# Mixture of experts on float32 weights as loaded, two column halves of TensorE at a time

## The chip, the cores and the metric

The program runs on one core of one Trainium2 chip. Its time is device microseconds of that core, from launch to end; the profiled execution beside it is one run of the same program taken by the hardware profiler. All times below are microseconds (us) from the start of the span unless marked ns.

## The reference

Two blocks run over 256 tokens of width 1024. The first block is two layers of FFN, mixer and FFN. The second has a mixer (block attention and gated linear attention) and then the mixture of experts that this change is about:

```
logits = norm(x) @ w_router + b_router            # 32 experts, the 4 largest per token
for each expert e, on the tokens that chose it:
    h      = norm(x) @ w_exp_in[e] + b_exp_in[e]  # 1024 -> 2048, gate and linear units in turn
    g, u   = min(h[0::2], 7), clip(h[1::2], -7, 7)
    a      = g * sigmoid(1.702 g) * (u + 1)       # 1024
    y     += softmax weight * (a @ w_exp_out[e] + b_exp_out[e])   # 1024 -> 1024
out = final_norm(x + gate * y)
```

All numbers are float32, and the result must agree with a float32 computation closely. The weights of one expert are 12 MiB: 8 MiB in, 4 MiB out. 32 experts are 384 chunks of 1 MiB, 403 MB.

## The kernel before

All weights pass through one stream (class `Stream`): chunks of 128 partitions x 2048 float32 (1 MiB), issued on SP's queue into raw places, in the order in which TensorE will use them. `convert` splits half a chunk into two float32r parts that add up to it: ScalarE writes the high part `wh` (L284), VectorE the rest `wl` (L285). The parts stand in a ring of five pairs (pool `hl`). When the second half of a chunk is split, its raw place is free and `load` issues the next chunk into it.

In the dense stages both operands are split, and a product is three float32r products (`prod`, L347 to L349). In the experts each expert has 64 slots for tokens. `Group.gather` (L1475) picks the tokens of four experts by products with a one-hot matrix and keeps the high and low part of each slot side by side, so the stationary operand is 64 + 64 columns wide. `hidden` multiplies it with `wh` and `wl` of a quarter of the hidden units (L1536, L1537; 64 products per expert), which leaves the two parts of x in two halves of the PSUM rows. `folded` adds the halves while it transposes, with a product by two stacked identities (L1549); VectorE and ScalarE do the bias, the limits and the sigmoid; L1564 and L1565 split the result into `act`. `outputs` does the same with the second matrix (L1579, L1580; 32 products per expert), ScalarE copies the sum to `osb` (L1584), and `combine` (L1523) adds each token's weighted rows into four PSUM banks `y` with a float32 product.

The order is written out by hand: the loop over `q` emits one quarter of an expert's hidden units and one quarter of the outputs of an expert some five quarters earlier; `later(PRE, n, ...)` and `later(POST, n, ...)` put the copies and the small products n steps further on, before or after that step's conversions. Raw places: three (`raw`), four (`r0` to `r3`) that join before the last dense product, and two (`xth`, `xtl`) used once when the dense stage is over. Up to five half chunks of the first expert are converted while the dense stage still runs.

The router's own chain stands between the dense stage and the experts: norm, logits, the four largest, places, one-hot matrix, gather. After the last expert `gated_sum` (L1607, L1608), the last norm and two stores end the program.

Of the kernel before, what the change touches and what calls it, by code (L numbers as in the profile page):

```python
# [23 lines left out]
OUT_ORDER = [*range(4 * NE - 3), 4 * NE - 2, 4 * NE - 3, 4 * NE - 1]  # L24
# [3 lines left out]
# ---------------------------------------------------------------- weight stream  # L28
# [77 lines left out]
# ---------------------------------------------------------------- constants of the shapes  # L106
def constants():
    f = np.float32
    c = {}
# [38 lines left out]
    c["fold"] = np.concatenate([np.eye(64, dtype=f)] * 2)  # L148
# [5 lines left out]
# ---------------------------------------------------------------- data layout on the host  # L154
def cols(v):
    """[..., 128 n] -> [128, ..., n]: a vector as columns of 128."""
    v = np.asarray(v)
    return np.ascontiguousarray(np.moveaxis(v.reshape(*v.shape[:-1], -1, 128), -1, 0))


def layout(a):
    o = {}
    parts = []
    for ch in dense_chunks():
# [5 lines left out]
        a["w_exp_in_2"][0].reshape(NE, 2, 4, 128, 4, 256, 2).transpose(0, 4, 1, 3, 2, 6, 5)  # L170
    ).reshape(NE, 4, 2, 128, 2048)
    o["exp_out"] = np.ascontiguousarray(
        a["w_exp_out_2"][0].reshape(NE, 2, 4, 128, 2, 512).transpose(0, 4, 1, 3, 2, 5)
    ).reshape(NE, 2, 2, 128, 2048)
    o["exp_bias"] = np.ascontiguousarray(
        a["b_exp_in_2"][0].reshape(NE, 2, 4, 128, 2).transpose(3, 0, 1, 4, 2)).reshape(128, NE, 16)
# [24 lines left out]
# ---------------------------------------------------------------- the program  # L201
def build(tc, I, out):
# [26 lines left out]
    # persistent  # L229
# [22 lines left out]
    # ------------------------------------------------ weight stream  # L252
    class Stream:
        """Weight chunks: loaded whole, split into two exact float32r parts by halves, and given out by halves."""

        def __init__(self, chunks, raw, hl):
            self.ch, self.raw, self.hl = chunks, [(raw, "raw")] * RAW, [hl] * HL
            self.d = self.c = self.u = self.step = 0
            self.R, self.C = {}, {}
            self.pre, self.post = [], []  # L260
            self.side = self.units = None
            self.hold = False

        def load(self, parts=1):
            if self.d < len(self.ch):
                ap, w = self.ch[self.d]
                p, tag = self.raw[0]
                self.raw = self.raw[1:] + self.raw[:1]
                r = p.tile([128, 2048], FT, name="raw", tag=tag)
# [6 lines left out]
                self.d += 1  # L276

        def convert(self):
            i, h = divmod(self.c, 2)
            r, w = self.R[i], self.ch[i][1] // 2  # L280
            p = self.hl[self.c % len(self.hl)]
            hi = p.tile([128, 1024], FR, name="wh")
            lo = p.tile([128, 1024], FR, name="wl")
            A.activation(hi[:, :w], r[:, h * w:h * w + w], AF.Copy)  # L284
            V.tensor_tensor(lo[:, :w], r[:, h * w:h * w + w], hi[:, :w], OP.subtract)  # L285
            self.C[self.c] = (hi, lo)
            self.c += 1
            if h:
                del self.R[i]
                self.load()  # L290

        def more(self, p, tags, once=False):
            """Further places for raw chunks, filled at once and, unless once, again in their turn."""
            for tag in tags:
                self.raw.insert(0, (p, tag))
                self.load()
                if once:
                    self.raw.pop()

        def due(self, q):  # L300
            now = [f for n, f in q if n <= self.step]
            q[:] = [(n, f) for n, f in q if n > self.step]
# [3 lines left out]
        def later(self, q, n, f):  # L306
            q.append((self.step + n, f))
# [7 lines left out]
        def fill(self):  # L315
            while self.c < min(self.u + len(self.hl), 2 * len(self.ch)):
                self.convert()

        def get(self):
            self.step += 1  # L320
            self.due(self.pre)
            if not self.hold:
                self.fill()
            self.due(self.post)
            if self.u % 2 == 0:
                if self.units:
                    self.units.step()
# [23 lines left out]
    def mm_tok(ps, X, klist, w, last, mid=None):  # L351
        """ps[t] += X[k]^T W[k] for the k of a chunk; mid comes between the chunk's halves."""
# [11 lines left out]
    def wide(p, X, lo=0, hi=8):  # L364
        """p [128 outputs, 256 tokens] += W[k]^T X[k] for the k of half a chunk."""
# [5 lines left out]
    def rms_power(o, ss, scale, eps):  # L371
        """o = (ss * scale + eps) ** -0.5"""
# [17 lines left out]
    raw = enter("raw", RAW)  # L390
    hl = enter("hl", HL)
# [22 lines left out]
    # ---------------------------------------- side work of the first block, a piece per chunk  # L414
# [59 lines left out]
    # ---------------------------------------- natural -> transposed stationary parts  # L474
# [3 lines left out]
    def turned(src, k, n=2):  # L478
        """A bank with (src columns k .. k+n)^T, [128, n, 256]."""
# [7 lines left out]
    def make_xt(X, src, half, gcol=None, after=None):  # L487
        """X[k] = (src columns k)^T * gcol for the four k of a half."""
# [17 lines left out]
    def rms_of(ss, eps, name="rstd", pre=None):  # L506
        """(mean + eps) ** -0.5 from the halves' sums of squares, which pre scales first."""
# [8 lines left out]
    class Norm:  # L516
        """The normed, transposed x of the next stage, in two halves of the columns."""
# [18 lines left out]
    # ---------------------------------------- FFN  # L536
# [74 lines left out]
    # ---------------------------------------- units of softmax work, stepped between chunks  # L611
    class Steps:
        """Units under way take one stage per chunk, the oldest first; one new unit starts per chunk."""
# [12 lines left out]
        def finish(self):  # L626
            while self.step():
                pass
            st.units = None

    # ---------------------------------------- first mixer
    def mixer(l, norm, next_gain):
# [16 lines left out]
        # -- Fourier branch between the projections  # L649
# [17 lines left out]
        def row_rstd(dg):  # L667
            """rstd along the free dimension, on every partition"""
# [61 lines left out]
        # -- attention, in steps between the chunks of the values and the gates  # L730
# [53 lines left out]
        def diff_unit(h, qt):  # L784
# [39 lines left out]
            # the heads' norms; their gain comes with the transposition  # L824
# [18 lines left out]
        st.units = att  # L843
# [29 lines left out]
        # -- branch outputs, gated and merged  # L873
# [36 lines left out]
        # -- output projection  # L910
# [15 lines left out]
    # ---------------------------------------- second mixer  # L926
# [865 lines left out]
```

## Time and profile before

| | |
|---|---|
| runs (3) | 2688.55, 2688.78, 2688.78 us; median 2688.78 |
| profiled execution, span | 2688.0 us, 34842 instructions |
| what the runs have around the span | 0.6 to 0.8 us |
| busy over the span: TensorE, VectorE, ScalarE, GpSimd | 97%, 77%, 64%, 7% |
| DMA | 712.89 MB, mean 265 GB/s |
| granted TensorE clock, mean | 0.994 |

How to read it: PE is TensorE, PEld its weight loads, DVE VectorE, ACT ScalarE, POOL GpSimd, SP the queue that issues loads. A matmul's busy time overlaps with the next one's, so the pace of TensorE is read from the distance of starts, and its busy share says little. The shares are averages over stages with different limits: the experts run from about 1626 us to the end, the dense stages before.

### The profile page before, as it was taken

To read this page: it belongs to the slowest core of one execution; us is meant where nothing else is said; L and a number is where in the kernel's file an instruction comes from. 1 tells how busy PE (TensorE), PEld (TensorE's weight loads), DVE (VectorE), ACT (ScalarE), POOL (GpSimd) and SP (SyncE) were. 2 spreads that over 40 slices of the span, in tenths; PEclk is the share of its full clock that TensorE was granted. 3 is DMA by queue.
4 is the path that set the end of the run, shared out by engine and by line. 5 is a ranking of instruction groups with operands and counts; after the bars stand their busy time and mean duration, and the time that the engine had idled before them with its cause. 6 is when DMAs were issued, how large, how long until landed. Compare 5 with 4: busy or idle time off the path is not lost.

```text
span 2688.0 us, 34842 instructions
## 1 busy us (share of the span) xinstructions
PE 2605.0 (97%) x12700; PEld 2092.6 (78%) x12700; DVE 2080.7 (77%) x2717; ACT 1723.2 (64%) x2290; POOL 182.6 (7%) x255
## 2 busy tenths in 40 slices
PE   8999999999999999999999998999999999999996
PEld 6889888887787978778798886777777777777775
DVE  5656766666666676655656679999999999999997
ACT  5444554444444454544555538989898989888886
POOL 1000000001101000000000102000000000000000
PEclk9999999999999999999999999999999999999999
DMA  7655445655566444565444566999999999999995
GB/s 282 220 216 207 153 149 192 221 218 211 213 225 245 149 153 172 193 226 180 158 149 151 175 246 251 381 399 389 381 393 388 386 388 391 388 393 389 390 395 203
DMA packets 106227, 712.89 MB, mean 265 GB/s; under 512 B 13380, under 2 KB 14052, under 8 KB 25409
## 3 DMA queue, kind: packets, MB, share of 16 engines
q1 hardware_dynamic: 92976, 667.03, 65.9%
q0 software_dynamic: 12928, 43.05, 4.3%
q8 instruction: 101, 1.65, 0.2%
q14 instruction: 78, 0.63, 0.1%
q10 hardware_dynamic: 144, 0.52, 0.0%
HBM read 709.40 MB, written 3.77 MB: 265 GB/s over the span
## 4 chain that ended last, share of the span: by engine, by line
PE 84%; DVE 9%; issue 3%; ACT 3%; DMA 0%; POOL 0%; DVEq 0%; SPq 0%; ACTq 0%; POOLq 0%
PE hid L1536 7%; PE hid L1537 6%; DVE wl L285 6%; PE po L1580 3%; PE pf L1549 3%; PE g L347 3%; PE u L347 3%; PE g L348 3%; PE u L349 3%; PE g L349 3%; PE u L348 3%; PE d L347 3%; PE d L349 3%; PE d L348 3%; PE y L1523 3%
## 5 line engine op out<-in xcount | busy, mean ns | idle before, releaser
L285 DVE TENSOR_TENSOR wl<-raw,wh 128x1024 fp32r<-128x1024 f32 (+2 forms) x1274 | 1504.7, 1218 | 424.7 <-ACT wh L284 414.9
L284 ACT ACTIVATE wh<-raw 128x1024 fp32r<-128x1024 f32 (+2 forms) x1274 | 1294.3, 1050 | 527.7 <-PE d L349 126.5
L1536 PE MATMUL hid<-wh,xgt 128*128 128x512 f32 x1024 | 441.0, 431 | 0.2 <-ACT hs L1539 0.2
L1537 PE MATMUL hid<-wl,xgt 128*128 128x512 f32 x1024 | 404.8, 395 | 0.0
L1580 PE MATMUL po<-wl,act 128*128 128x512 f32 x512 | 208.6, 407 | 32.9 <-DVE wl L285 32.9
L1536 PEld LDWEIGHTS hid<-wh,xgt 128*128 128x128 f32 x1024 | 193.3, 189 | 54.3 <-issue 16.1
L1537 PEld LDWEIGHTS hid<-wl,xgt 128*128 128x128 f32 x1024 | 193.3, 189 | 53.3 <-issue 14.3
L1579 PE MATMUL po<-wh,act 128*128 128x512 f32 x512 | 204.0, 398 | 2.8 <-ACT osb L1584 2.8
L1580 PEld LDWEIGHTS po<-wl,act 128*128 128x128 f32 x512 | 96.1, 188 | 78.5 <-DVE wl L285 57.6
L347 PE MATMUL g<-wh,xth 128*128 128x512 f32 (+1 forms) x384 | 147.0, 383 | 0.0
L347 PE MATMUL u<-wh,xth 128*128 128x512 f32 (+1 forms) x384 | 146.0, 380 | 0.0
L348 PE MATMUL g<-wl,xth 128*128 128x512 f32 (+1 forms) x384 | 144.8, 377 | 0.0
L349 PE MATMUL g<-wh,xtl 128*128 128x512 f32 (+1 forms) x384 | 144.5, 376 | 0.0
L349 PE MATMUL u<-wh,xtl 128*128 128x512 f32 (+1 forms) x384 | 144.4, 376 | 0.0
L348 PE MATMUL u<-wl,xth 128*128 128x512 f32 (+1 forms) x384 | 144.1, 375 | 0.0
L347 PE MATMUL d<-wh,hth 128*128 128x512 f32 x352 | 139.8, 397 | 0.0
L349 PE MATMUL d<-wh,htl 128*128 128x512 f32 x352 | 138.8, 394 | 0.0
L348 PE MATMUL d<-wl,hth 128*128 128x512 f32 x352 | 138.8, 394 | 0.0
L1549 PEld LDWEIGHTS pf<-fold,hs 128*128 128x128 f32 x1024 | 130.8, 192 | 8.8 <-issue 1.3
L1549 PE MATMUL pf<-fold,hs 128*128 128x64 f32 x1024 | 129.1, 269 | 1.4 <-DVE v L1555 0.9
L1523 PE MATMUL y<-osb,ohw 128*128 128x512 f32 x256 | 123.0, 603 | 2.1 <-ACT osb L1584 2.1
L1493 POOL TENSOR_TENSOR wdup<-oh,wgt 128x128 f32<-128x128 f32 x64 | 72.5, 1162 | 741.4 <-PE wts L1500 510.0
(488 smaller groups left out, 4441.6 us busy)
## 6 DMA issues: line engine op xcount, KB each, us to landing
raw<-d_exp_in SPq DMA_DIRECT2D x256, 1024.0 KB, 7.3
raw<-d_dense SPq DMA_DIRECT2D x245, 1024.0 KB, 4.8
raw<-d_exp_out SPq DMA_DIRECT2D x128, 1024.0 KB, 7.5
ada_w<-d_ada POOLq DMA_DIRECT2D x96, 256.0 KB, 4.6
bias<-tables POOLq DMA_DIRECT2D x2, 1920.0 KB, 12.7
bg<-d_b_gate POOLq DMA_DIRECT2D x12, 256.0 KB, 4.2
raw<-d_dense SPq DMA_DIRECT2D x4, 768.0 KB, 4.5
raw<-d_dense SPq DMA_DIRECT2D x5, 512.0 KB, 3.6
```

What stands on the lines that cost most here:

```text
L284: A.activation(hi[:, :w], r[:, h * w:h * w + w], AF.Copy)
L285: V.tensor_tensor(lo[:, :w], r[:, h * w:h * w + w], hi[:, :w], OP.subtract)
L347: T.matmul(ps, lhsT=xh, rhs=wh, start=start, stop=False)
L348: T.matmul(ps, lhsT=xh, rhs=wl, start=False, stop=False)
L349: T.matmul(ps, lhsT=xl, rhs=wh, start=False, stop=stop_)
L1493: G.tensor_tensor(d[:, :, c], oh, wg, OP.mult)
L1523: T.matmul(y[t][n], lhsT=grp[e // 4].w[:, e % 4, t], rhs=osb[e, n], start=e == 0, stop=e == NE - 1)
L1536: T.matmul(ph, lhsT=lhs, rhs=wh[:, 512 * i:512 * i + 512], start=k == 0, stop=False)
L1537: T.matmul(ph, lhsT=lhs, rhs=wl[:, 512 * i:512 * i + 512], start=False, stop=k == 7)
L1549: T.matmul(pf[:, 4 * (c // 2) + 2 * (j % 2) + c % 2], lhsT=hs[:, 128 * c:128 * c + 128], rhs=fold, start=True, stop=True)
L1579: T.matmul(po, lhsT=lhs, rhs=wh[:, 512 * i:512 * i + 512], start=k == 0, stop=False)
L1580: T.matmul(po, lhsT=lhs, rhs=wl[:, 512 * i:512 * i + 512], start=False, stop=k == 7)
```

## The change

The expert weights are used as they were loaded. `convert` ends with the dense chunks; in the experts `Stream.whole` hands out a raw chunk and lets the one before it go. A slot matrix is 64 columns of float32, and `both` issues two products with it, one into PSUM rows 0 to 63 and one into rows 64 to 127, each with its own 512 columns of weights. The hidden units come in two halves per expert instead of four quarters, the fold becomes a plain transpose, `act` is one float32 tile, and `combine` takes the two row halves of `osb`. The copies stand directly behind the products that they wait for. Freed tiles of the dense stage (`c0` to `c4`, `xtl`, `xth`) and one new place (`rx`) become raw places for good. The small weighting products go from GpSimd to ScalarE, and the last two rows (gate and final norm) go from GpSimd's queue to SP's, into a raw place. The host lays the expert weights out to match. Comments are dropped. The rest of the program is as before.

```diff
     class Stream:
         def __init__(self, chunks, raw, hl):
-            self.ch, self.raw, self.hl = chunks, [(raw, "raw")] * RAW, [hl] * HL
+            self.ch, self.raw, self.hl = chunks, [(raw, f"raw{i}") for i in range(RAW)], [(hl, f"c{i}") for i in range(HL)]
+            self.units = [(i, h) for i in range(DENSE) for h in range(2)]
...
+        def place(self):
+            p, tag = self.raw.pop(0)
+            return (p, tag), p.tile([128, 2048], FT, name="raw", tag=tag)

         def load(self, parts=1):
-            if self.d < len(self.ch):
+            while self.raw and self.d < len(self.ch):
                 ap, w = self.ch[self.d]
-                p, tag = self.raw[0]
-                self.raw = self.raw[1:] + self.raw[:1]
-                r = p.tile([128, 2048], FT, name="raw", tag=tag)
+                self.T[self.d], r = self.place()
...
+        def done(self, i):
+            del self.R[i]
+            self.raw.append(self.T.pop(i))
+            self.load()

         def convert(self):
...
-            hi = p.tile([128, 1024], FR, name="wh")
-            lo = p.tile([128, 1024], FR, name="wl")
+            both = p.tile([128, 2048], FR, name="w", tag=tag)
+            hi, lo = both[:, :1024], both[:, 1024:]
...
+        def whole(self):
+            if self.last is not None:
+                self.done(self.last)
+            self.last = DENSE if self.last is None else self.last + 1
+            self.step += 1
+            self.due()
+            return self.R[self.last]
...
-    for q in range(4 * NE + 5):
-        if q < 4 * NE:
-            dense += [(I["exp_in"][q // 4, q % 4, h], 2048) for h in range(2)]
-        if q >= 5:
-            e, j = divmod(OUT_ORDER[q - 5], 4)
-            dense.append((I["exp_out"][e, j // 2, j % 2], 2048))
+    for q in range(2 * NE + 1):
+        if q < 2 * NE:
+            dense += [(I["exp_in"][q // 2, 4 * (q % 2) + m], 2048) for m in range(4)]
+        if q:
+            dense += [(I["exp_out"][(q - 1) // 2, 2 * ((q - 1) % 2) + m], 2048) for m in range(2)]
...
-        st.more(xtp[0], ("xth", "xtl"), once=True)
+        st.more(hl, [f"c{i}" for i in range(HL)])
+        st.more(xtp[0], ("xtl", "xth"))
...
+        st.more(enter("rx", 1), ("rx",))
...
-                        G.tensor_tensor(d[:, :, c], oh, wg, OP.mult)
+                        A.activation(d[:, i], rep(oh[:, SL * (e + i):SL * (e + i + 1)], 2, 1), AF.Copy,
+                                     scale=wgt[:, t, n:n + 1])
...
-        def combine(e, n, t):
-            T.matmul(y[t][n], lhsT=grp[e // 4].w[:, e % 4, t], rhs=osb[e, n], start=e == 0, stop=e == NE - 1)
+        def combine(e):
+            for t in range(2):
+                for n in range(2):
+                    r = slice(64 * n, 64 * n + 64)
+                    T.matmul(y[t][n], lhsT=grp[e // 4].w[r, e % 4, t], rhs=osb[e][r], start=e == 0, stop=e == NE - 1)
+
+        def both(ps, x, w, c, start, stop_):
+            for n in range(2):
+                T.matmul(ps[64 * n:64 * n + 64], lhsT=x, rhs=w[:, 1024 * c + 512 * n:1024 * c + 512 * n + 512],
+                         start=start, stop=stop_)

-        def hidden(e, j):
+        def hidden(e, a, between):
             X = grp[e // 4].x
             ph = hbank("hid")
-            for h in range(4):
-                wh, wl = get()
...
+            for m in range(4):
+                if e + a == 0 and m < 3:
+                    grp[0].gather(2 * m + 2, y[(m + 1) // 2][(m + 1) % 2])
+                w = st.whole()
+                for c in range(2):
+                    both(ph, X[:, 2 * m + c, e % 4], w, c, m + c == 0, m + c == 4)
+                between()
             hs = w2.tile([128, 512], FT, name="hs")
-            later(PRE, 1, lambda: A.activation(hs, ph, AF.Copy))
-            later(POST, 3 if e < NE - 1 or j < 3 else 2, lambda: folded(e, j, hs))
+            A.activation(hs, ph, AF.Copy)
+            later(2, lambda: activate(e, a, hs))
...
+        def outputs(e, m):
+            if m == 0:
+                pos_[0] = pop.tile([128, 512], FT, name="po")
+            po = pos_[0]
+            w = st.whole()
+            for c in range(2):
+                both(po, act[e][:, 4 * (m // 2) + 2 * c + m % 2], w, c, m + c == 0, m + c == 4)
+            if m == 3:
+                osb[e] = w2.tile([128, 512], FT, name="osb")
+                A.activation(osb[e], po, AF.Copy)
                 if e < NE - 1:
-                    later(PRE, 1, lambda: A.activation(osb[e, n], po, AF.Copy))
-                    later(POST, 3, lambda: [combine(e, n, t) for t in range(2)])
+                    later(2, lambda: combine(e))
```

## Rows read from the trace of the kernel before

**Rows 1.** Table by stage: busy us and instructions of each engine, clock, DMA.

```profile
core 0: us, PE busy (x) PEld busy (x) DVE busy (x) ACT busy (x) POOL busy (x), PEclk, DMA share, GB/s
1600.00:1650.00 50.00, 41.53 (x218) 34.48 (x216) 42.47 (x68) 35.62 (x54) 9.82 (x9) 0.90 0.64 235
1650.00:1700.00 50.00, 46.72 (x234) 37.10 (x235) 49.53 (x57) 45.30 (x60) 10.06 (x8) 1.00 0.84 328
...
1800.00:2600.00 800.00, 771.50 (x3597) 594.03 (x3595) 791.42 (x898) 715.42 (x900) 51.35 (x47) 1.00 0.99 390
```

**Rows 2.** Groups by line, 1800 to 2600 us: the two conversions.

```profile
L285 DVE TENSOR_TENSOR wl<-raw,wh 128x1024 fp32r<-128x1024 f32 x592 | 688.8, 1220 | 5.2 <-ACT wh L284 1.3
...
L284 ACT ACTIVATE wh<-raw 128x1024 fp32r<-128x1024 f32 x593 | 592.2, 1051 | 4.8 <-PE hid L1536 4.2
```

**Rows 3.** Waits, 1700 to 2640 us: us in total, times, longest; SP's, TensorE's.

```profile
SPq L272 <- DVE wl L285: 677.3, 284, 4.5
...
PEld po L1580 <- DVE wl L285: 53.8, 56, 2.3
```

**Rows 4.** Raw chunks, issue to landing: 2000 to 2640 us; 1655; the last load.

```profile
DMA to landing us min/median/max: 5.8/7.4/9.1
...
DMA to landing us min/median/max: 4.8/4.8/4.8
...
L272 SPq DMA_DIRECT2D raw<-d_exp_out x1: 328/328/328, 2646.6 to 2646.6; - x1
...
DMA to landing us min/median/max: 7.4/7.4/7.4
```

**Rows 5.** The first expert loads, and the table of the 14 us behind them.

```profile
L272 SPq DMA_DIRECT2D raw<-d_exp_in x5: 328/422/656, 1585.1 to 1587.2; - x5
...
DMA to landing us min/median/max: 4.8/8.7/12.5
...
1590.00:1604.00 14.00, 14.00 (x66) 11.39 (x65) 10.62 (x12) 5.21 (x6) 0.00 (x0) 1.00 1.01 425
```

**Rows 6.** Timeline of TensorE, several pieces: start, duration, instruction.

```profile
2000.36 0.40 PE L1536 MATMUL hid<-wh,xgt 128*128 128x512 f32 x1
2000.36 0.19 PEld L1537 LDWEIGHTS hid<-wl,xgt 128*128 128x128 f32 x1
2000.59 0.39 PE L1537 MATMUL hid<-wl,xgt 128*128 128x512 f32 x1
...
2003.19 0.19 PEld L1523 LDWEIGHTS y<-osb,ohw 128*128 128x128 f32 x1 [0.24 <-issue]
2003.62 0.19 PEld L1536 LDWEIGHTS hid<-wh,xgt 128*128 128x128 f32 x1 [0.24 <-issue]
...
1611.20 1.07 PE L1361 MATMUL tp<-head,z 128*128 128x128 f32 x8
```

**Rows 7.** Timeline of TensorE: float32 products on two row halves, then on one.

```profile
280.59 0.28 PE L349 MATMUL qk<-xth,wl 128*128 128x256 f32 x1
280.80 0.70 PE L790 MATMUL fsc<-qk 64*128 64x256 f32 x4
281.43 0.50 PE L347 MATMUL v<-wh,xth 128*128 128x512 f32 x1
281.77 0.39 PE L348 MATMUL v<-wl,xth 128*128 128x512 f32 x1
...
334.55 1.56 PE L757 MATMUL dsc<-qk 64*128 64x256 f32 x6
336.04 0.50 PE L347 MATMUL z<-wh,xth 128*128 128x512 f32 x1
```

**Rows 8.** Timeline: the last dense product, the first expert product, the end.

```profile
1609.24 0.40 PE L349 MATMUL o<-wh,xtl 128*128 128x512 f32 x1
...
1626.29 0.65 PE L1536 MATMUL hid<-wh,xgt 128*128 128x512 f32 x1
...
2671.42 0.69 DVE L1607 TENSOR_TENSOR osb<-y,fin 128x512 f32<-128x512 f32 x1 [5.31 <-PE y L1523]
```

More of the change, by code (lines that the diff above doesn't have):

```diff
@@ L276, in load, with more, rows @@
                 self.d += 1
+                if self.d <= RAW:
+                    break
+        def done(self, i):
+            del self.R[i]
+            self.raw.append(self.T.pop(i))
+            self.load()
+        def more(self, p, tags):
+            for tag in tags:
+                self.raw.insert(0, (p, tag))
+                self.load()
+        def rows(self, srcs):
+            _, r = self.place()
+            for i, src in enumerate(srcs):
+                SP.dma_start(r[:, 1024 * i:1024 * i + 1024], src)
+            return r[:, :1024], r[:, 1024:]
         def convert(self):
[L279 removed]
+            i, h = self.units[self.c]
             r, w = self.R[i], self.ch[i][1] // 2
[L281 to L285 removed]
+            p, tag = self.hl.pop(0)
+            self.hl.append((p, tag))
+            both = p.tile([128, 2048], FR, name="w", tag=tag)
+            hi, lo = both[:, :1024], both[:, 1024:]
+            r = r[:, h * w:h * w + w]
+            A.activation(hi[:, :w], r, AF.Copy)
+            V.tensor_tensor(lo[:, :w], r, hi[:, :w], OP.subtract)
             self.C[self.c] = (hi, lo)
@@ L288, in convert, with due, later @@
             if h:
[L289 to L302, printed above, removed]
+                self.done(i)
+        def due(self):
+            now = [f for n, f in self.todo if n <= self.step]
+            self.todo = [(n, f) for n, f in self.todo if n > self.step]
             for f in now:
                 f()
-        def later(self, q, n, f):
-            q.append((self.step + n, f))
+        def later(self, n, f):
+            self.todo.append((self.step + n, f))
         def start(self):
@@ L1462, in __init__ @@
                 self.oh = w2.tile([128, 2, 256], FR, name="oh") if g else router.oh
-                p, tags = ((xgp, ("xga", "xgb")), (xtp[0], ("xth", "xtl")))[g % 2]
-                self.x = [p.tile([128, 4, 4, 2, SL], FR, name="xgt", tag=tag) for tag in tags]
+                self.x = xgp.tile([128, 8, 4, SL], FT, name="xgt")
                 self.w = w2.tile([128, 4, 2, 128], FT, name="ohw")
-                self.todo = [lambda k=k: later(PRE, 1, self.gather(k)) for k in range(8 if g else 0)] + \
+                self.todo = [lambda k=k: self.gather(k, hbank("gat")) for k in range(0, 8 if g else 0, 2)] + \
                             [lambda e=e: self.weights(e) for e in (0, 2)]
@@ new lines, in combine @@
+        def combine(e):
+            for t in range(2):
+                for n in range(2):
[5 more added lines that the diff above has]
+                         start=start, stop=stop_)
@@ L1527, in hidden @@
+        def hidden(e, a, between):
             X = grp[e // 4].x
             ph = hbank("hid")
-            for h in range(4):
-                wh, wl = get()
-                if e + j == 0 and h in (1, 2):
-                    grp[0].pair(2 * h + 2)
-                for i in range(2):
-                    k = 2 * h + i
-                    lhs = X[k // 4][:, k % 4, e % 4].rearrange("p c s -> p (c s)")
-                    T.matmul(ph, lhsT=lhs, rhs=wh[:, 512 * i:512 * i + 512], start=k == 0, stop=False)
-                    T.matmul(ph, lhsT=lhs, rhs=wl[:, 512 * i:512 * i + 512], start=False, stop=k == 7)
@@ L1561, in folded @@
[L1561 to L1582 removed]
+            V.tensor_tensor(act[e][:, 4 * a:4 * a + 4], v[:, 4:8], sg, OP.mult)
@@ L1613, in squares @@
             A.activation(junk, x[:, t, 512 * n:512 * n + 512], AF.Square, accum_out=ss[:, 2 * n + t:2 * n + t + 1])
-        for q in range(4 * NE + 5):
-            e, j = divmod(q, 4)
+        grp[0].gather(0, y[0][0])
+        for q in range(2 * NE + 1):
+            e, a = divmod(q, 2)
+            g = e // 4 + 1
             if q == 1:
                 router.weigh()
-            if q == 17:
-                later(POST, 1, bias_part)
-            if q in (20, 22):
-                later(POST, 1, lambda: bias_sum(q // 2 - 10))
-            if q == 12:
+            if q == 6:
@@ L1646, in moe, with between @@
-        for t in range(2):
-            for n in range(2):
-                combine(NE - 1, n, t)
+            if q == 9:
+                later(1, bias_part)
+            if q in (10, 11):
+                later(1, lambda: bias_sum(q - 10))
+            if q == 13:
+                leave("bp")
+            if q == 2 * NE:
+                fin.extend(st.rows((bcast_row(mods, D, 3 * D), bcast_row(I["final_norm"], D))))
+            def between():
+                if q in (2, 3):
+                    grp[0].step()
+                if e % 4 >= 1 and g < NE // 4:
+                    grp[g].step()
@@ L1649, in moe @@
+            if e < NE:
+                if e % 4 == 1 and a == 0 and g < NE // 4:
+                    grp[g] = Group(g)
+                if a == 0:
+                    act[e] = actp.tile([128, 8, SL], FT, name="act")
+                hidden(e, a, between)
+            if q:
+                for m in range(2):
+                    outputs((q - 1) // 2, 2 * ((q - 1) % 2) + m)
+        while st.todo:
+            st.step += 1
+            st.due()
+        combine(NE - 1)
         for t in range(2):
```

193 lines of the change are left out of this document (60 added, 133 removed).

## The prediction

> **What bounds the kernel now.** I read the table by stage first, then the groups by line of the expert stage, then the waits of the queue that loads, then the landings of the loads.
>
> The table by stage [rows 1] shows two kernels in one. From 1800 to 2600 us the DMA engines are busy 0.99 of the time at 390 GB/s and VectorE 99%; between 1600 and 1700 us the same engines idle at 235 and 328 GB/s. The groups [rows 2] say what VectorE does there: 592 subtractions `wl` of 1.22 us in 800 us, 688.8 us of 791. An expert has 24 of them, so an expert takes 800 x 24 / 592 = 32.4 us, 29.3 us of it in `wl`; 12 chunks of 1 MiB in 32.4 us are 2.70 us a chunk. SP's waits [rows 3] agree: it holds nearly every load back for a place, and the place is let go by `wl` (677 us). TensorE waits for `wl` (53.8 us), and no compute engine waits for a load.
>
> So is it VectorE or the DMA? A lone chunk lands 4.8 us after its issue; in the expert stage none lands before 5.8 us and the median is 7.4 [rows 4]. The transfers always have a backlog of about one chunk, so 2.70 us a chunk is also close to what the DMA then delivers. But when five loads were issued at once (1585.1 us) the same queue ran 14 us at 425 GB/s [rows 5]: 1.0486 MB / 425 = 2.47 us a chunk. Both are near their limits; taking VectorE away makes the DMA the bound, and the question is only at which of 2.47 and 2.69 us a chunk (390 GB/s).
>
> **The change part by part.**
>
> *Removed.* In the experts 768 `wl` and 768 `wh` conversions (1.22 us on VectorE, 1.05 on ScalarE). What else VectorE does is 791.4 - 688.8 us in 24.7 experts [rows 1, 2], 4.2 us each; ScalarE's other work is (715.4 - 592.2) / 24.7 = 5.0 us, to which two small products per expert come from GpSimd. Both are far under 30 us, so all their edits cost nothing; without that cover each would cost its duration.
>
> *TensorE, the dear term.* 96 float32r products per expert at 0.23 us (starts 2000.36, 2000.59 in [rows 6]) become 48 float32 products. A float32 product of 512 columns shows as two records, and each takes 0.43 us (the weight load of `y` starts at 2003.19, the next at 2003.62 [rows 6]). 96 records one after the other would be 41.3 us; two at a time 20.6. The trace of before has no pair of column halves, so I bound it: above by no overlap at all (41.3), below by full overlap (20.6). The nearest row is a pair of row halves: `fsc`, four float32 records on rows 0 to 63 and 64 to 127, lets the next group start 0.63 us after its first (280.80 to 281.43), 0.16 a record; `dsc`, six records on one half only, needs 1.49 (334.55 to 336.04), 0.25 a record [rows 7]. A change of shape costs about 0.2 us in both: `fsc` starts 0.21 us after the last full-size record of 256 columns in place of 0.12 (280.59, 280.80), and the record behind it takes 0.34 in place of 0.23 (281.43, 281.77). Without it that is 0.11 a record against 0.215: full overlap. I take 20.6 and keep both ends.
>
> The rest of TensorE per expert: the weighted sum, 8 records of 0.43 on two row halves, 1.7 us; 8 transposes, 1.0 (8 in 1.07 us [rows 6]); 8 gather records of half the columns of a `hid` record, 0.9; weight transposes 0.3; about eight changes of shape at 0.2, 1.6. Sum 26.1 us per expert. 12 chunks at 2.47 are already 29.6: TensorE hides under the DMA with 3 to 6 us to spare.
>
> The Trainium skill speaks against this part: its page "TensorE: Matmul & The Clock Gate", section "Part 3: Packing small matmuls — row/col tiling", says that a weight load runs beside a product only where the row group differs, and column halves share all rows. By that rule nothing overlaps, which is the third rival below; the trace only half agrees, since the load of 2000.36 us runs beside a product on the same rows [rows 6]. The same section measured 2.38 for three column tiles; two tiles at the same share of the ideal (2 x 2.38 / 3 = 1.59) make an estimate of 41.3 / 1.59 = 26 us in place of 20.6, and 1626.3 + 32 x 31.5 + 21.1 = 2655 us in all.
>
> *Places.* Before, 9 places hold raw chunks ahead, two of them once only. After, 15: three raw, four r, five c (once the dense stage has let them go), xtl, xth, rx. The first load is issued at 1585.1 and lands at 1589.9 in both kernels. Before, the queue then stands still for places: in [rows 1] it lacks 36% and 16% of two 50 us stretches. After, seven loads run as now (to about 1605), the c and xt places come by the last dense product (1609.24 [rows 8]), and the first expert product starts as now, about 1626.3 [rows 8], because gather needs the same router chain. Fifteen chunks last from 1590 to about 1625, so the queue stands still once, for 5 to 7 us (late c places, or all 15 full until the first is read). I take 6.
>
> *Rate afterwards.* TensorE empties places faster than they are filled, so soon up to a dozen loads stand in the queue and it never runs dry. That is nearest to [rows 5], 2.47; the other end is 2.69. I take 2.52, leaning to the burst, with a little for whatever else the queues carry. Last landing: 1589.9 + 6 + 383 x 2.52 = 2561.
>
> *Tail.* Before, the last load lands at 2646.6 + 7.4 = 2654.0 [rows 4] and 34 us follow, since a queue of conversions and products is still to be done. After, behind the last landing: two pairs (1.9 us with a semaphore), the copy of `po` (0.6 and 0.1), the first half of the sum (1.2), and from there VectorE's chain unchanged, 2671.42 to 2688.0 = 16.6 [rows 8]. Sum 20.4. The two rows for the end (1 MiB) now ride SP's queue behind the last chunk, 2.5 us later than it, needed 3.8 us later: hidden; at worst 3 us.
>
> *The rest.* The dense stages keep their products, conversions and places; hi and lo now share one tile, but ScalarE waited for the last product of a half anyway, so I set 0 (bounds -3 to +3, less than two chunks).
>
> Sum: 2561 + 20.4 = 2581.5 of span, against 2688.0 before; the runs lie 0.6 to 0.8 above the span: **2582 us**, 4.0% faster.
>
> **The rivals.**
>
> *The DMA gives no more than now.* The 390 GB/s at a share of 0.99 [rows 1] would then be what the transfers give beside three busy engines, however long their queue. For it: the backlog of [rows 4] never empties. Against it: [rows 5], 14 us with TensorE full. Then 1589.9 + 6 + 383 x 2.69 + 20.4 + 0.7 = 2647 us.
>
> *TensorE becomes the bound and the gain shrinks.* With X us per expert the end is 1626.3 + 32 X + 21.1. It passes the DMA's 2582 at X = 29.2 and before's time at 32.6. Imperfect overlap or dearer changes of shape at 30 to 32 give 2607 to 2671.
>
> *Column halves don't run side by side: slower.* The place is `both`, the price up to 0.43 us on each of 48 pairs of records, the deciding point X = 32.5, which is 0.13 us lost on each pair. Weight loads of 0.19 us laid bare there give 26.1 + 9.1 = 35.2, 2774 us; no overlap gives 46.8, 3145 us. For it: no column pair in the trace. Against it: [rows 7]. This is also the case that the change doesn't do what it says.
>
> **How the numbers follow.** Forecast, DMA-bound at 2.47 to 2.6 us a chunk (2563 to 2613): 0.56. DMA as now: 0.14. TensorE between: 0.14. Slower: 0.14. The remaining 0.02 is a gain of the places alone, eaten elsewhere. A change under 0.2% can't be told from none; that band (2683 to 2694) gets 0.03 from the second rival's upper end, so faster 0.83, same 0.03, slower 0.14. The range 2550 to 2668 takes in the first, the second and most of the third case, and leaves 0.2 out, nearly all above.
>
> **What would show it.** In the expert stage of after: VectorE under 20%; DMA share about 1.0 at 405 to 425 GB/s from 1610 us on; SP waiting for `hid` and `po` products, in the steady stage TensorE waiting for loads; landings far over 7.4 us, as the queue is long. Pairs of `hid` records with equal starts, 0.43 us from pair to pair, show the overlap; starts 0.43 apart one by one show the slower rival. TensorE with no waits for loads shows the second rival, 390 GB/s with long landings the first. An end more than 25 us behind the last landing proves the tail wrong. The granted clock should stay 1.00: TensorE idles only some 0.3 us a chunk.

## The result, and the profile after

| | before | after |
|---|---|---|
| median of 4 runs | 2688.78 us (2688.55 to 2692.11) | 2579.59 us (2578.70 to 2583.44) |
| ratio | | 0.9593, 95% interval 0.9579 to 0.9606 |
| profiled execution, span | 2688.0 us | 2581.7 us |

The profiled execution of after is the longest of its four runs (2583.44). Its first 100 us explain that, so they come first in the table by stage. The columns are those of [rows 1].

```profile
20.00:30.00 10.00, 8.31 (x21) 5.16 (x20) 5.63 (x10) 5.92 (x14) 1.29 (x2) 0.66 0.56 218
1600.00:1650.00 50.00, 43.48 (x223) 28.00 (x223) 22.73 (x52) 15.68 (x29) 4.95 (x5) 0.90 0.87 350
1650.00:1700.00 50.00, 48.63 (x240) 18.98 (x238) 8.37 (x22) 13.97 (x33) 0.00 (x0) 1.00 1.01 413
1800.00:2500.00 700.00, 633.77 (x2860) 206.59 (x2858) 101.15 (x250) 91.34 (x189) 0.00 (x0) 1.00 1.01 421
```

Against [rows 1], 235, 328 and 390 GB/s have become 350, 413 and 421, and VectorE is busy 14% of the expert stage (101 of 700 us) in place of 99%. The first line is a disturbance: from 20 to 30 us the clock granted was 0.66, where before had 1.00. It put the rest of this execution about 3 us later ("Did the dense stages lose 3 us?" below).

The waits answer to [rows 3]: engine, line, what was waited for; us in total, times, longest, here from 1700 to 2500 us. First all engines, then SP's queue.

```profile
DVE v L1561 <- PE pf L1559: 677.1, 55, 15.4
PEld hid L1537 <- DMA raw<-d_exp_in: 138.0, 121, 2.5
...
SPq L274 <- DMA raw<-d_exp_in: 435.8, 209, 3.2
SPq L274 <- DMA raw<-d_exp_out: 217.5, 104, 2.4
SPq L274 <- PE hid L1537: 18.4, 27, 3.4
```

The direction of waiting has turned round. TensorE now waits for loads (before, for `wl`), VectorE waits for TensorE, and SP hardly waits for a reader of a place (18.4 us). It waits for a DMA: a load is issued when the eighth load before it has landed (0.06 us after it, in the median), since the program gives the loads eight semaphores in turn. The landing times say the same: median 19.8 us from issue, eight chunks at 2.49.

```profile
DMA to landing us min/median/max: 11.7/19.8/21.0
```

TensorE's weight loads stand in for the starts that [rows 6] gave (start, duration, count):

```profile
2004.84 0.14 PEld L1537 LDWEIGHTS hid<-raw,xgt 128*64 128x64 f32 x2 [0.28 <-issue]
2005.27 0.14 PEld L1537 LDWEIGHTS hid<-raw,xgt 128*64 128x64 f32 x2 [0.28 <-issue]
2005.70 0.14 PEld L1537 LDWEIGHTS hid<-raw,xgt 128*64 128x64 f32 x2 [0.29 <-issue]
```

Two records every 0.43 us, the time of one record in [rows 6]: the overlap of the two column halves is complete. The start and the end of the expert stage, as SP issued it, with the first of VectorE's last chain, which answers to 2671.42 in [rows 8]:

```profile
1588.12 24.93 SPq L274 DMA_DIRECT2D raw<-d_exp_in  x8
1613.10 0.90 SPq L274 DMA_DIRECT2D raw<-d_exp_out  x2
1614.04 2.15 SPq L274 DMA_DIRECT2D raw<-d_exp_in  x4
1624.77 7.46 SPq L274 DMA_DIRECT2D raw<-d_exp_out  x2
...
2541.19 0.33 SPq L274 DMA_DIRECT2D raw<-d_exp_out  x1
...
2564.83 0.69 DVE L1600 TENSOR_TENSOR osb<-y,raw 128x512 f32<-128x512 f32 x1 [6.37 <-PE y L1532]
```

The first chunk is issued at 1588.1 and lands at 1593.0; the last is issued at 2541.2 and lands 19.8 us later, at 2561.0; the end is 20.7 us behind it.

### The profile page after: what moved, and what is told of

Read it like the earlier page. It is cut to its first block, busy times and chain, and to the rows that moved or that the text cites. A ratio compares the mean times of both kernels' runs of the same rounds, so it can differ in the third digit from the quotient of the medians.

```text
span 2581.7 us, 30105 instructions
## 1 busy us (share of the span) xinstructions
PE 2463.4 (95%) x11932; PEld 1610.5 (62%) x11932; DVE 1186.8 (46%) x1885; ACT 924.1 (36%) x1394; POOL 108.1 (4%) x188
## 5 line engine op out<-in xcount | busy, mean ns | idle before, releaser
L310 DVE TENSOR_TENSOR w<-raw,w 128x1024 fp32r<-128x1024 f32 (+1 forms) x506 | 609.6, 1213 | 416.0 <-ACT w L309 412.4
L309 ACT ACTIVATE w<-raw 128x1024 fp32r<-128x1024 f32 (+1 forms) x506 | 526.9, 1048 | 521.1 <-PE u L369 129.4
L1537 PE MATMUL hid<-raw,xgt 128*64 128x512 f32 x2048 | 481.7, 601 | 48.8 <-DMA raw<-d_exp_in 48.5
L1537 PE MATMUL po<-raw,act 128*64 128x512 f32 x1024 | 247.0, 602 | 25.8 <-DMA raw<-d_exp_out 24.8
L367 PE MATMUL g<-w,xth 128*128 128x512 f32 (+1 forms) x384 | 147.2, 383 | 0.0
L367 PE MATMUL u<-w,xth 128*128 128x512 f32 (+1 forms) x384 | 147.0, 383 | 0.0
L369 PE MATMUL u<-w,xtl 128*128 128x512 f32 (+1 forms) x384 | 145.4, 379 | 0.0
L368 PE MATMUL u<-w,xth 128*128 128x512 f32 (+1 forms) x384 | 145.1, 378 | 0.0
L368 PE MATMUL g<-w,xth 128*128 128x512 f32 (+1 forms) x384 | 144.9, 377 | 0.0
L369 PE MATMUL g<-w,xtl 128*128 128x512 f32 (+1 forms) x384 | 144.5, 376 | 0.0
L367 PE MATMUL d<-w,hth 128*128 128x512 f32 x352 | 139.8, 397 | 0.0
L368 PE MATMUL d<-w,hth 128*128 128x512 f32 x352 | 138.8, 394 | 0.0
L367 PE MATMUL z<-w,xth 128*128 128x512 f32 x288 | 115.8, 402 | 0.0
L368 PE MATMUL z<-w,xth 128*128 128x512 f32 x288 | 113.8, 395 | 0.0
## 6 DMA issues: line engine op xcount, KB each, us to landing
raw<-d_exp_in SPq DMA_DIRECT2D x256, 1024.0 KB, 19.8
raw<-d_exp_out SPq DMA_DIRECT2D x128, 1024.0 KB, 19.8
```

The source lines that it names most:

```text
L309: A.activation(hi[:, :w], r, AF.Copy)
L310: V.tensor_tensor(lo[:, :w], r, hi[:, :w], OP.subtract)
L367: T.matmul(ps, lhsT=xh, rhs=wh, start=start, stop=False)
L368: T.matmul(ps, lhsT=xh, rhs=wl, start=False, stop=False)
L369: T.matmul(ps, lhsT=xl, rhs=wh, start=False, stop=stop_)
L1537: T.matmul(ps[64 * n:64 * n + 64], lhsT=x, rhs=w[:, 1024 * c + 512 * n:1024 * c + 512 * n + 512], start=start, stop=stop_)
```

## The experiments

The theory: before, VectorE's `wl` held the places and so the loads, and the DMA ran below its rate of 421 GB/s; after, nothing but the DMA binds in the expert stage, because two column halves run side by side and TensorE fits beneath the transfers. Rivals: 390 GB/s was what transfers get beside busy engines or with few loads under way; TensorE binds too; the overlap has another cause. Medians, and ratios to the kernel before on the same chip:

| run | us | ratio, 95% interval | GB/s, 1800 to 2400 us |
|---|---|---|---|
| e1_same_half | 2967.13 | 1.103, 1.1012 to 1.1049 | 303 |
| e2_half_loads | 2473.09 | 0.9197, 0.9181 to 0.9212 | 245 |
| e3_busy | 3109.01 | 1.156, 1.1541 to 1.158 | 278 |
| e3b_busy | 2590.83 | 0.9636, 0.962 to 0.9652 | 421 |
| e4_no_low | 2629.93 | 0.9778, 0.9761 to 0.9794 | 413 |
| e5_places8 | 2596.17 | 0.9655, 0.9639 to 0.9672 | 421 |
| e6_places5 | 2607.65 | 0.9696, 0.968 to 0.9713 | 420 |
| e9_queues | 2581.04 | 0.96, 0.9584 to 0.9616 | 421 |
| e12_again | 2578.84 | 0.9586, 0.9573 to 0.9599 | 421 from 1800 to 2500 |
| e10_four_lost | 2587.24 | 0.9619, 0.9606 to 0.9632 | 420 |
| e8_places16 | 2575.77 | 0.9577, 0.9564 to 0.959 | 421 from 1800 to 2500 |
| e11_gate | 2572.74 | 0.9564, 0.9551 to 0.9578 | 421 from 1800 to 2500 |

### Does the overlap come from the column halves?

```diff
             for n in range(2):
-                T.matmul(ps[64 * n:64 * n + 64], lhsT=x, ...
+                r = 64 * n if start or stop_ else 0
+                T.matmul(ps[r:r + 64], lhsT=x, ...
```

> The changed kernel, but in each accumulation over eight pairs the six inner pairs send both products into PSUM rows 0 to 63 (the first and last pair keep their two halves), so the second column half of the sums is left incomplete. Work and transfers are the same. Theory (two products share the array because they stand in different column halves): 36 of an expert's 48 pairs of records fall apart, 36 x 0.43 = 15.5 us more per expert, 26.1 + 15.5 = 41.6; TensorE becomes the bound, end = 1629.5 + 32 x 41.6 + 21 = 2982 us; the starts of these records stand 0.43 us apart one by one, DMA falls to about 300 GB/s. Rival (float32 records follow each other 0.215 us apart whatever rows they write): no change, 2580 us.

2967 us, and the weight loads in one accumulation, the first pair still in two halves:

```profile
2002.57 0.19 PEld L1538 LDWEIGHTS hid<-raw,xgt 128*64 128x64 f32 x2
2003.05 0.14 PEld L1538 LDWEIGHTS hid<-raw,xgt 128*64 128x64 f32 x1 [0.29 <-issue]
2003.48 0.14 PEld L1538 LDWEIGHTS hid<-raw,xgt 128*64 128x64 f32 x1 [0.29 <-issue]
2003.91 0.14 PEld L1538 LDWEIGHTS hid<-raw,xgt 128*64 128x64 f32 x1 [0.29 <-issue]
```

One record per 0.43 us where the rows are the same, two where they differ. The span gives (2965.9 - 1627.9 - 21) / 32 = 41.2 us per expert; the 2982 that was expected is 15 us too high for the 41.6 and the later start in it. The rival is out.

### How fast is TensorE alone?

```diff
-            if self.last is not None:
-                self.done(self.last)
-            self.last = DENSE if self.last is None else self.last + 1
+            if self.step % 2 == 0:
+                if self.last is not None:
+                    self.done(self.last)
+                self.last = DENSE if self.last is None else self.last + 1
...
+    dense[DENSE:] = dense[DENSE::2]
```

> The changed kernel, but each expert chunk is used twice and every second one is not loaded: 192 chunks, same TensorE work. Shows TensorE's own pace. Theory (26.1 us per expert, hidden with some 3 us to spare): 1629.5 + 32 x 26.1 + 21 = 2486 us, TensorE waits for no load after the first ones, DMA about 240 GB/s. Rival (TensorE barely fits, 29 us or more per expert, and the time of the changed kernel is its pace as much as the DMA's): 2578 us or more.

2473 us; span 2470.5, first `hid` at 1625.24: (2470.5 - 1625.2 - 21) / 32 = 25.8 us per expert. The trace says the same without the assumed end: the copies `osb` repeat every 103.1 us per four experts. The 2486 that was expected is too high by the pace (26.1) and by the start (1629.5). With half the bytes TensorE binds:

```profile
1800.00:2400.00 600.00, 600.00 (x2836) 213.81 (x2834) 99.13 (x245) 90.38 (x187) 0.00 (x0) 1.00 0.67 245
```

So TensorE has 12 x 2.49 - 25.8 = 4.1 us to spare per expert in the changed kernel. A later run spends most of that:

```diff
-        def both(ps, x, w, c, start, stop_):
+        def both(ps, x, w, c, start, stop_, same=False):
...
-                T.matmul(ps[64 * n:64 * n + 64], lhsT=x, ...
+                r = 0 if same else 64 * n
+                T.matmul(ps[r:r + 64], lhsT=x, ...
...
-                    both(ph, X[:, 2 * m + c, e % 4], w, c, m + c == 0, m + c == 4)
+                    both(ph, X[:, 2 * m + c, e % 4], w, c, m + c == 0, m + c == 4, m == 1)
```

> The changed kernel with 4 of an expert's 24 pairs of products (the third and fourth of each half of the hidden units) sent into the same PSUM rows, so that they no longer overlap; those sums are left incomplete. TensorE's pace rises from 25.7 us per expert by 8 x 0.43 to 29.1, still under the 29.9 of the transfers. Theory (TensorE's time below the transfers' is free): 2580 to 2590 us, 415 to 421 GB/s from 1800 us on. Rival (TensorE and the transfers share the time, so each us more per expert shows at least in part): half of 32 x 3.4, 55 us, or more: 2635 us or later.

2587 us, 8.4 more than the changed kernel beside it (2578.84). This is within the theory's numbers, but not free, and the run does not stand well below the border. Its copies `osb` repeat every 116.7 us per four experts, 29.2 us each, and by the prediction's 1626.3 + 32 X + 21.1 that ends at 2582 us, its own border between TensorE and the loads. TensorE hardly waits for loads any more (1800 to 2400 us; the changed kernel, e12, then e10):

```profile
PEld hid L1537 <- DMA raw<-d_exp_in: 108.2, 96, 2.3
...
PEld hid L1538 <- DMA raw<-d_exp_in: 6.2, 14, 0.8
```

The loss sits early; after 1800 us the rate is 420 GB/s again.

```profile
1650.00:1700.00 50.00, 48.62 (x218) 19.24 (x216) 7.27 (x20) 13.32 (x32) 0.00 (x0) 1.00 0.95 374
```

In that stretch e12 moves 416 GB/s, and from 1600 to 1650 us 350 against 334: together 2.9 MB, or 7 of the 8.4 us. TensorE begins with all places full and has to empty them faster than they fill before the queue can run ahead; with 29.9 - 29.2 = 0.7 us to spare per expert that takes long. The waits agree: from 1626 to 1800 us SP waits for products of TensorE alone in e10, while e12 waits mostly for its eight loads from 1700 us on. That this is the whole cause was not isolated.

### Is 390 GB/s the price of busy engines?

```diff
+            for _ in range(1 + self.step % 2):
+                A.activation(self.dh, x[:, 0], AF.Copy)
+                V.tensor_tensor(self.dl, x[:, 0], self.dh, OP.subtract)
...
-        st.more(enter("rx", 1), ("rx",))
+        rx = enter("rx", 1)
+        st.dh, st.dl = rx.tile([128, 1024], FR, name="dh"), rx.tile([128, 1024], FR, name="dl")
```

> The changed kernel with VectorE and ScalarE kept busy by 18 subtractions and 18 copies of 128 x 1024 per expert that nothing waits for (x into a scratch tile that takes the room of one raw place). VectorE 18 x 1.22 + 4.2 = 26 us, ScalarE 18 x 1.05 + 4 = 23 us of an expert's 29.9. Theory (390 GB/s before came from a queue that ran dry, not from busy engines): DMA stays at 415 to 421 GB/s in the expert stage, the time rises by the missing place alone, 2.5 us, to 2582 to 2588. Rival (busy engines cost the transfers their rate): 390 GB/s, 1 MiB in 2.69 us, 384 x 0.19 = 73 us more, about 2650.

3109 us, and neither side had this. The waits (columns as above, 1800 to 2400 us):

```profile
DVE dl L352 <- ACT dh L351: 251.6, 234, 2.6
ACT dh L351 <- DVE dl L352: 242.7, 202, 1.6
PEld pf L1563 <- ACT hs L1556: 152.5, 26, 11.4
```

The two engines waited for each other through one scratch tile, the copy `hs` stood behind that in ScalarE's queue, and TensorE waited for `hs` up to 11.4 us. It then also got less clock: 0.84 over 1800 to 2400 us. The DMA was 71% busy, so the run says nothing of its rate. It was repeated with the two engines unlinked:

```diff
-                V.tensor_tensor(self.dl, x[:, 0], self.dh, OP.subtract)
+                V.tensor_tensor(self.dl, x[:, 0], x[:, 1], OP.subtract)
```

> As the busy run before it, but the two engines no longer wait for each other: 18 copies of 128 x 1024 per expert on ScalarE (x into scratch) and 18 subtractions on VectorE (one half of x minus the other into another scratch tile) that no instruction of another engine waits for. Theory (390 GB/s came from a queue that ran dry): DMA 415 to 421 GB/s in the expert stage, one place less costs 2.5 us, the copies of sums may come some us later: 2580 to 2590 us. Rival (busy VectorE and ScalarE cost the transfers their rate): 390 GB/s, about 2650 us.

```profile
1650.00:1700.00 50.00, 45.25 (x210) 18.22 (x208) 39.83 (x45) 39.29 (x59) 0.00 (x0) 0.93 0.87 332
1800.00:2500.00 700.00, 638.38 (x2880) 209.84 (x2878) 622.97 (x681) 530.72 (x621) 0.00 (x0) 1.00 1.01 421
```

VectorE 89% and ScalarE 76% busy, and 421 GB/s all the same. The 2591 us are just outside the expected range, some 9 us more than the missing place explains. They are lost before 1700 us (332 GB/s against 413 in this stretch, four chunks or 10 us). There SP waits for products of TensorE alone, so the loads are short of places, not of rate (1640 to 1700 us):

```profile
SPq L274 <- PE hid L1541: 31.0, 13, 9.7
```

TensorE in turn is late: from 1650 to 1660 us it is busy 5.9 of 10 us, it waits for small results of the two busy engines (2.9 us for `oh` before one gather), and its granted clock is 0.81 and 0.85 in the two stretches of 10 us from 1650 on. Which of these costs how much was not isolated.

### Was it VectorE that held before back?

In the kernel before, one part alone:

```diff
-            lo = p.tile([128, 1024], FR, name="wl")
             A.activation(hi[:, :w], r[:, h * w:h * w + w], AF.Copy)
-            V.tensor_tensor(lo[:, :w], ...
+            lo = hi
+            if i < len(dense_chunks()):
+                lo = p.tile([128, 1024], FR, name="wl")
+                V.tensor_tensor(lo[:, :w], ...
```

> The kernel before without its 768 subtractions wl in the experts: the products with the low part use the high part again (so the low parts of the expert weights are left out of the result). Places, order, TensorE's products and ScalarE's copies as before. Theory (VectorE held the places and so the loads): per expert the next bounds are DMA 29.9 us and ScalarE 24 x 1.05 + 5 = 30.2, so 32.4 falls to 30.2 to 30.8, 31 experts x 1.6 to 2.2 = 50 to 68 us less: 2620 to 2639 us, 410 to 420 GB/s. Rival (390 GB/s is all that the transfers give with these places and engines): 2680 to 2689 us, 390 GB/s.

2630 us, 58 less than before, with before's places and TensorE work, and a last landing at 2596.6 in place of 2654.0:

```profile
1800.00:2400.00 600.00, 600.00 (x2862) 475.62 (x2861) 99.52 (x244) 559.01 (x716) 14.89 (x40) 1.00 1.01 413
```

The theory's numbers. The next engine, ScalarE, is at 93% (559 of 600 us), and SP now waits for it alone, as it did for VectorE before (1800 to 2400 us):

```profile
SPq L272 <- ACT wh L283: 427.8, 197, 2.8
SPq L272 <- ACT act L1566: 88.6, 39, 2.3
```

That this is what keeps the rate 2% under 421 was not tested by itself.

### Does the long queue of loads give the rate?

```diff
-        st.more(hl, [f"c{i}" for i in range(HL)])
-        st.more(xtp[0], ("xtl", "xth"))
```

> The changed kernel with 8 raw places in the expert stage in place of 15 (c0 to c4, xtl and xth are not added). Theory (places count only until TensorE starts, afterwards the rate is the DMA's): the 9th chunk lands when the 16th does now, near 1637, and 375 chunks at 2.50 us follow it in place of 368: 14 us more than the changed kernel, 2594 us, and still 418 to 421 GB/s from 1800 us on. Rival (the long queue of loads gives the 421): about as before with its 7 to 9 places, 390 to 400 GB/s, 2640 to 2660 us.

In the run with 5 places (e6), `more(p2, ...)` also adds only `r2` and `r3`, and `rx` is not added.

> The changed kernel with 5 raw places (raw0 to raw2, r2, r3). Theory: the 6th chunk lands near 1637, 378 chunks follow: 22 us more than the changed kernel, 2601 us; one place is read, so four loads at most are under way, which covers TensorE's longest absence (weighted sum and transposes, 4 us) with a little loss: 410 to 421 GB/s, 2601 to 2625 us. Rival (a long queue gives the rate): under 400 GB/s, 2650 us or more.

2596 and 2608 us, and 421 and 420 GB/s after 1800. With five places the median landing is 10.3 us, about four chunks under way (five places less the one being read), and that is enough:

```profile
DMA to landing us min/median/max: 4.8/10.3/11.9
```

From 15 to 8 places each costs 2.4 us ((2596.2 - 2579.6) / 7), one chunk; from 8 to 5 it is 3.8, somewhat more than expected (412 GB/s still from 1700 to 1800). With 8 places SP again waits for readers nearly all the time, as in the kernel before (1800 to 2400 us):

```profile
SPq L274 <- PE hid L1535: 306.9, 157, 3.4
```

So a queue that waits for places need not lose rate; what counts is that the reader lets them go faster than the chunks land. Places are worth what they hold before TensorE begins, not a rate.

```diff
-                    SP.dma_start(r[:, sl], ap[:, sl])
+                    (G if self.d >= DENSE + RAW and self.d % 2 else SP).dma_start(r[:, sl], ap[:, sl])
```

> The changed kernel with every second expert chunk issued on GpSimd's queue in place of SP's. Theory (the 16 DMA engines are full at a share of 1.0, 421 GB/s is their rate): 421 GB/s, no change, 2578 to 2584 us. Rival (one queue with eight loads under way is the limit): more than 430 GB/s, 2 to 3 us less per 1% of rate above 421.

2581 us, 421 GB/s. With two queues more loads are under way (34.9 us to landing, 14 chunks: fifteen places less the one being read), and nothing comes of it:

```profile
DMA to landing us min/median/max: 25.7/34.9/37.0
```

### Did the dense stages lose 3 us?

> The changed kernel once more, as the yardstick for the three beside it: 2579 to 2581 us. In the profiled run theory says that the first expert load is issued at 1584 to 1585 us where the granted clock from 20 to 30 us is 1.00, and some 3 us later where it dips as in the first profile (0.66): the dense stages themselves cost what they did. Rival (the shared tile for high and low part delays them): 1587 to 1588 at any clock.

```profile
20.00:30.00 10.00, 10.00 (x42) 7.13 (x41) 6.22 (x10) 6.35 (x12) 1.29 (x2) 1.00 0.51 195
...
1585.24 24.92 SPq L274 DMA_DIRECT2D raw<-d_exp_in  x8
```

No dip, and the first expert load at 1585.24, where before had 1585.07 [rows 5]. Of the twelve traces of the changed kernel and its variants the two with a dip there (0.66 and 0.83) have it at 1588.1 and 1586.7, the ten others, all at 1.00, at 1583.8 to 1585.2. The delay of the first profile is there right behind its dip and stays as it is: its last dense load is issued at 1581.65, here at 1578.77. The shared tile costs nothing. The median, 2578.84, lies 0.2 us under the expected 2579 to 2581.

### A better one

```diff
-        st.more(hl, [f"c{i}" for i in range(HL)])
+        st.more(hl, [tag for _, tag in st.hl])
...
+        w1 = enter("ew1", 1)
...
-        st.more(enter("rx", 1), ("rx",))
+        st.more(enter("rx", 1), ("rx", "ry"))
...
-            hs = w2.tile([128, 512], FT, name="hs")
+            hs = w1.tile([128, 512], FT, name="hs")
...
```

> An attempt at a better one: 16 raw places (room from single buffers for hs, v, sg, osb) and the five dense tiles join in the order in which they come free (c1, c2, c3, c4, c0 in place of c0 to c4). Theory (each place filled before TensorE starts is worth one chunk, 2.5 us; the order closes the gap between the loads of 1600 and 1613 us but the places are then full until the first chunk is read, worth 0.8 us): 3.3 us less than the changed kernel, 2576 us. Rival (the stand-still of 7 us after 1605 us comes off in full): 10 us less, 2570 us. Rival on the other side (the single buffers make TensorE wait): 2580 us or more.

2575.8 us beside 2578.8, 3.1 less: the theory's number. The new order closes the first gap (the eighth load is issued at 1596.6 in place of 1612.7 in the first profile), and the queue then waits further on for the first chunk to be read:

```profile
1584.05 12.89 SPq L274 DMA_DIRECT2D raw<-d_exp_in  x8
1599.38 3.13 SPq L274 DMA_DIRECT2D raw<-d_exp_out  x2
1604.98 5.68 SPq L274 DMA_DIRECT2D raw<-d_exp_in  x4
1610.89 10.19 SPq L274 DMA_DIRECT2D raw<-d_exp_out  x2
1627.17 3.34 SPq L274 DMA_DIRECT2D raw<-d_exp_in  x2
```

The place and the order came in one run. With 2.4 us for a place, from the run with 8 places, some 0.7 us are left for the order, which is within the scatter of the runs (2574.8 to 2576.9).

```diff
-                A.activation(osb[e], po, AF.Copy)
+                V.tensor_tensor(osb[e], po, gt, OP.mult)
...
-                V.tensor_tensor(tmp, y[t][n], fin[0][:, sl], OP.mult)
-                V.tensor_tensor(x[:, t, sl], x[:, t, sl], tmp, OP.add)
+                V.tensor_tensor(x[:, t, sl], x[:, t, sl], y[t][n], OP.add)
```

> The one before with a shorter end: each expert's output sum is multiplied by the gate where it is copied (VectorE in place of ScalarE, 0.7 us for 0.6), the bias rows too, so that behind the last load four additions of 0.69 us stand in place of four products and four additions. Theory: 4 x 0.69 = 2.7 us off the end, 2573 us. Rival (the copy waits on VectorE behind the sigmoid chain and TensorE's slack doesn't cover it): no gain or a loss, 2576 us or more.

2572.7 us, 3.0 less again, the fastest here that does all of the work: 0.9564 of before, and 6.1 us under the changed kernel run beside it. The four products are gone from the end:

```profile
2557.57 2.48 DVE L1605 TENSOR_TENSOR x<-x,y 128x512 f32<-128x512 f32 x4 [1.21 <-PE y L1538]
```

## Why the prediction was right

Forecast 2582, measured 2579.6. The mechanism held: the loads bind, at the rate of the old burst, with TensorE hidden beneath them. That the sum comes within 2.4 us is partly luck, since the stand-still was set too short and the time of a chunk too long.

- **What binds.** Right. Without `wl` alone the kernel before gains 58 of the 109 us and its DMA reaches 413 GB/s.
- **The rate.** Right, and my lean to the burst was not even far enough: (2561.0 - 1593.0 - 9.7) / 383 = 2.50 us a chunk in place of 2.52, which is 7 us over the stage. The rival with 2.69 is out: neither busy engines (e3b) nor few places (e6) bring 421 GB/s down by more than 1, and a second queue does not lift it.
- **TensorE.** 25.8 us per expert in place of 26.1, with full overlap at 0.43 us a pair. The Trainium skill (TensorE: Matmul & The Clock Gate, Part 3: Packing small matmuls — row/col tiling) says that a weight load runs beside a product only where the row group differs. This case's traces disagree, since pairs on the same 128 rows follow each other at 0.43 us, the pace of a single record. By itself that rule would lay weight loads bare, the 35.2 us of the third rival; the prediction took it for no overlap at all, which it does not say. The same section of the Trainium skill measured 2.38 for three column tiles, from which the prediction estimated 1.59 for two; measured here is 2.0.
- **The slower rival.** Its price was real, 15.4 us per expert for 36 pairs (41.2 - 25.8), but the case does not arise. TensorE binding in part would have begun where it was worked out, at 29.2: at 29.2 (e10) 8 us are lost.
- **Places.** Mis-sized, and half the reason was wrong. I set one stand-still of 6 us. In the trace the first chunk lands at 1593.0 and the sixteenth at 1637.5, 44.5 - 15 x 2.49 = 7.1 us lost, and the next one 2.5 us late: 9.7. The 7.1 are lost in one place, before the eighth load, which waits for `c0` until 1612.7 and lands 9.6 us behind the seventh (1607.9, 1617.5). Yet of the two causes that I named, late `c` places decide next to nothing: the order in which I read them out of the code, `c0` first, is the worst (`c0` is freed last), but with the right order the places are simply full until TensorE has read the first chunk, and the run with it (e8) leaves some 0.7 us for the order. "Up to a dozen loads" in the queue was wrong too; it is eight. The sign that SP would wait for `hid` and `po` products held only at the start of the experts; in the steady stage it waits for its own loads.
- **Dense stages.** Zero, as set; the 3 us of the first profile belong to its clock.
- **Tail.** 20.7 us, forecast 20.4.
- **Around the span.** Mis-sized. The 0.6 to 0.8 us can't be runs and span of the same execution. Where both are on record for one, the run is 1.7 to 2.0 us longer than its span (2583.44 and 2581.7 here), so this term was 1.1 us short.

Together, for the profiled execution: first landing 3.1 later, stand-still 3.7 longer, rate 6.9 less, last landing 2561.0 against a forecast of 2561. The undisturbed one (e12) has it at 2557.0 and a span of 2577.5, 4.0 us under the forecast span; with 1.1 us more around the span the median lies 2.4 us under the forecast.

Where the 110.5 us between the spans of before and the undisturbed run (2688.0, 2577.5) come from: 13.5 from the tail (34.0 to 20.5) and 97 from the last landing. Of these, what before still had to load after 1800 us, 854 us at 390 GB/s, takes 854 x 390 / 421 = 791: 63 us by the rate. The other 34 were won before 1800 us, where before loaded at 235 and 328 GB/s while its queue waited for places. About half of them are the added places: with 8 (e5) 17 us are lost again. The other half was not taken apart.

## What to carry to other kernels

When two resources are both near their limit, the question is at which rate the second stands once the first is gone; a short burst with a full queue in the old trace answered that to 1% (425 against 421 GB/s). Once a stage is bound by its loads, four things count most: the bytes, the first load, what is stored before the reader starts (one chunk's time per place), and what is left to do behind the last landing. An engine beneath the loads also needs time to spare to catch up after its late start: 4.1 us per expert were enough here, 0.7 were not. A test that loads an engine must not link it to another, or it measures the link.

## What the runs showed of the hardware that was not expected

- Two float32 products in the two column halves overlap entirely even though both read all 128 rows: 0.43 us a pair, exactly half the time of the same pair in one half.
- Four loads of 1 MiB under way are as good as 8 or 14: 420, 421 and 421 GB/s, and the time to landing is about their number times 2.49 us (10.3, 19.8, 34.9).
- VectorE at 89% and ScalarE at 76%, both on SBUF, cost the loads no rate: 421 GB/s from 1800 to 2500 us with them and without.
- TensorE paused for 9.6 us in e3, until 2003.3. The stretch of 10 us in which the pause ended was granted 0.55 of the clock (the lower level, 1.2 of 2.4 GHz, is 0.50), and the next one, with a pause of 2.7 us, 0.83:

```profile
2003.31 1.11 PE L1563 MATMUL pf<-head,hs 128*128 128x128 f32 x4 [9.58 <-ACT hs L1556]
...
2000.00:2010.00 10.00, 6.69 (x20) 2.34 (x20) 5.05 (x5) 5.14 (x6) 0.00 (x0) 0.55 0.35 139
2010.00:2020.00 10.00, 7.32 (x28) 2.54 (x28) 6.70 (x9) 4.08 (x6) 0.00 (x0) 0.83 0.53 193
```
